# First modulation sums moved to TensorE, rotary tables moved to the start

## The chip, the core and the metric

The kernel runs on one core of a Trainium2 chip. A core has TensorE (matrix products, called PE in the profile, with its weight loads as PEld), VectorE (DVE), ScalarE (ACT), GpSimd (POOL) and SyncE (SP), which here only issues DMA transfers. Each engine takes its own instructions in the order in which they are written and waits where an operand is not ready. The metric is the device time of one execution in microseconds (us), and the kernel is compared by the median of its runs.

## The reference, cut to what matters

A two-layer encoder trunk, sequence 512, model width 1024, all in fp32. Each layer first makes six modulation vectors from the conditioning vector c, then normalises the input, and reads it with one input projection that feeds three mixers:

```
c_act = jax.nn.silu(c)
for l in range(DEPTH):
    mod = c_act @ w_mod[l] + b_mod[l]
    sh1, sc1, g1, sh2, sc2, g2 = (m[:, None, :] for m in jnp.split(mod, N_MOD, axis=-1))
    h = rmsnorm(x, norm1[l]) * (1.0 + sc1) + sh1
    u = h @ w_in[l]
    ...
    x = x + g1 * (mixed @ w_out[l])
    h2 = rmsnorm(x, norm2[l]) * (1.0 + sc2) + sh2
    x = x + g2 * conv_ffn(h2, ffn_w_up[l], ffn_conv_w[l], ffn_conv_b[l], ffn_w_down[l])
```

`mod` has 6144 values per layer, 48 chunks of 128. Chunks 0 to 7 are the shift `sh1` and chunks 8 to 15 the scale `sc1`: no column of `h` can be made before its shift and its scale are there. Two of the mixers also need rotary tables, the cosines and sines of `positions` times fixed frequencies.

## The kernel before, in words

The activations lie transposed: the model dimension on 128 partitions in 8 rows of blocks (k = 0 to 7, `KD`), the 512 tokens along the columns. A product in full precision is made of three products of fp32r parts (`mm3`, lines 348 to 350): each weight tile is split into a high part `wh` (a cast on ScalarE, line 342) and a low part `wl` (a subtraction, line 343, on VectorE or GpSimd), and `h` likewise into two tiles named `t`.

The program is written as one text; a scheduler lays down the order of each engine from priorities (`PRI`, `low`, `after`) and its own costs. That order is fixed when the kernel is built.

What runs at the start of layer 0:

- `x` (tile `xs`), the columns of small parameters (`cols`), the constants (`cst`, in two parts, the first 265 KB on ScalarE's queue) and c (`crow`, on one partition) are loaded. c is activated on one partition and copied to all 128 by two products with ones (`spread`, tile `cb`, line 296) into `cact`.
- `x_norm` squares the 8 rows of `xs` on ScalarE (`nsq`, line 412), adds them on VectorE (`nacc`, line 421), sums over partitions on TensorE (`ssq`, line 391), takes the root on VectorE (`rs_y`, lines 356 to 365) and spreads it over the partitions by four transposes (`bc`, line 372).
- The first projection (`proj(0)`, six column blocks) goes over k. For each k, `make_h` makes two modulation sums by `mod_chunk`: a tile `rawm` of 512 KB (the weights of one chunk, transposed in memory) is multiplied by `cact` and summed along its columns in one VectorE instruction (line 327), which gives one column of `modv`. Three buffers serve `rawm`. Then the gain `g_n` (line 771), `ht` (line 440, VectorE), the high part of `t` (line 442, ScalarE) and its low part (line 443, VectorE). 18 products `u` per k follow.
- When the last k is done, six blocks of `u` are read out, four of them squared and summed (`dsq`, line 843). Beside the second projection (`proj(1)`, five blocks) run the preparation of the state-space mixer (lines 497 to 637) and the rotary tables: `rope_tables` (lines 466 to 488) loads the positions and makes `tabA`, `tabS` and `tabC` on VectorE, with four sines on ScalarE.

The weights of the projections are loaded to `raw` (three buffers), and SP issues the transfers of `rawm`, `raw` and the others in one fixed order: a transfer that waits for a buffer holds up all behind it. The PSUM tiles `ssq`, `bc` and others share two banks; `bc` keeps one of them until the last `ht` of layer 0's first projection.

The other 80 modulation sums are made later by the same VectorE instruction.

Of the kernel before, what the change touches and what calls it, by code (L numbers as in the profile page):

```python
# [20 lines left out]
D = 1024  # L21
# [3 lines left out]
PRI = {"xs": -400, "U1": 300, "ws": -200, "rs": -300, "cu": 10, "fin": 20, "glu": -30, "par": -30,  # L25
       "prep1": -20, "qk": 20, "rope": -20}
MK = 2
OWN = 6
TOGETHER = 300
DQ = (0, 3, 0, 0)  # L30
BLOCKS = ((0, 8), (8, 15), (15, 22))
EPS = 1e-6
# [23 lines left out]
for _name, _w in (  # L56
    ("ident", 128), ("ss", 12), ("fr", 6), ("nidx", 256), ("mf", 128), ("mb", 128),
    ("rz", 256), ("sel", 128), ("bias", 896),
):
    CONST[_name] = (_n, _w)  # L60
    _n += _w
# [9 lines left out]
def _constants():  # L71
    out = np.zeros((128, NCONST), np.float32)

    def put(name, a):
        o, w = CONST[name]
        out[:, o:o + w] = a

    p = np.arange(128)
    put("ident", np.eye(128))
    sel = np.zeros((128, 128))  # L80
    for j in range(32):
# [50 lines left out]
def _layout(inp):  # L132
    a = {k: np.asarray(v) for k, v in inp.items()}
    f = np.float32
    o = {}
    o["xT"] = a["x"][0].T.reshape(8, 128, N).transpose(1, 0, 2)
    o["c"] = a["c"].reshape(1, D)
    o["pos"] = a["positions"].reshape(1, N)
    o["const"] = _constants()
    o["wmod"] = a["w_mod"].transpose(0, 2, 1).reshape(L, 48, 128, D)  # L140
    cols = np.zeros((128, L, NCOL), f)
    rope = lambda g: np.concatenate([g[:16], g[16:], g[16:], g[:16]])
# [74 lines left out]
def program(ctx, tc, a, out):  # L217
# [41 lines left out]
    xs = keep.tile([128, KD, N], F32, name="xs")  # L259
    crow = strm.tile([128, 1024], F32, tag="raw", name="crow", bufs=3)  # L260
    S.dma_start(crow[:1], a["c"])
    nc.sync.dma_start(cols, a["cols"])
    for k in range(0, KD, 2):
        nc.sync.dma_start(xs[:, k:k + 2], a["xT"][:, k:k + 2])
    S.dma_start(cst[:, :NEARLY], a["const"][:, :NEARLY])

# [19 lines left out]


    cact = keep.tile([128, D], F32, name="cact")
    S.activation(cact[:1], crow[:1], AF.Tanh, scale=0.5)
    V.scalar_tensor_tensor(cact[:1], cact[:1], 1.0, crow[:1], add, mul)  # L290

    def spread():
        for i in range(2):
            o = ps("cb", "big")
            c = slice(i * 512, i * 512 + 512)
            T.matmul(o, K("mf")[:1], cact[:1, c], start=True, stop=True)
            S.copy(cact[:, c], o)

# [10 lines left out]

    def mod_chunk(l, j, pooled=False):  # L310
        with low("mod" if l or j >= 16 else "mod0"):
            mod_chunk_(l, j, pooled)

    def mod_chunk_(l, j, pooled=False):
        if cur["modraw"]:
            p_, nb = cur["modraw"]
            r = p_.tile([128, 1024], F32, tag="rawm", name="rawm", bufs=nb)
            nc.sync.dma_start(r, a["wmod"][l, j])
        else:
            r = raw_tile(a["wmod"][l, j], 1024)  # L320
        if pooled:
            G.tensor_tensor(r, r, cact, mul)
            acc = tiny("modacc", 1, bufs=4)
            S.activation(r, r, AF.Copy, scale=0.5, accum_out=acc)
            G.tensor_tensor(modv[l][:, j:j + 1], acc, col(l, "bmod", j), add)
        else:
            V.tensor_tensor_reduce(out=r, in0=r, in1=cact, scale=0.5, scalar=col(l, "bmod", j),  # L327
                                   op0=mul, op1=add, accum_out=modv[l][:, j:j + 1])

# [418 lines left out]
    def mixing(l, background):  # L748
# [7 lines left out]
        if l == 0:  # L756
            g1 = keep.tile([128, 8], F32, name="g_n10")
            start = startup(pst)
            with low("par"):
                next(start, None)  # L760
            *_, R = x_norm(slice(0, N), True)
            ready = cur["rs"]
            cur["H"] = [(ht(2 * k), ht(2 * k + 1)) for k in range(KD)]
        H = cur["H"]

        def make_h(k):
            with after(*[cur["ht"]] if k else ()):
                mod_chunk(0, 8 + k)
            with after(cur["ht"] if k else ready):
                mod_chunk(0, k)  # L770
            V.tensor_scalar(g1[:, k:k + 1], modv[0][:, 8 + k:9 + k], 1.0, col(0, "n1", k), op0=add, op1=mul)
            normed(R, g1, modv[0][:, 0:8], k, slice(0, N))
# [7 lines left out]
        def proj(gi, o):  # L780
# [3 lines left out]
            for k in range(KD):  # L784
# [3 lines left out]
                for i0 in range(0, nt, 3):  # L788
                    i1 = min(nt, i0 + 3)
                    wh, wl = split(r[:, i0 * 128:i1 * 128], (i1 - i0) * 128,  # L790
                                   G if (i0 == 0 or l + gi == 0) else V)
                    for i in range(i0, i1):
                        c = slice((i - i0) * 128, (i - i0) * 128 + 128)
                        mm3(o[i], (wh[:, c], wl[:, c]), H[k], k == 0, k == KD - 1)
# [86 lines left out]
        with ExitStack() as st:  # L881
            if l == 0:
                cur["modraw"] = (pool("early", "right", st), 3)
            if l:
# [16 lines left out]
        if l == 0:  # L901
# [11 lines left out]
            pst.close()  # L913
            with low("rope"):
                rope_tables()
        dil_roots(0, 32)
# [557 lines left out]
    banks("pa", cur["pst"], big=6, ps=2)  # L1474
    spread()
    open_norm()
# [33 lines left out]
```

## Time and profile before

| | |
|---|---|
| median of 3 runs | 1508.67 us (1507.85 to 1509.09) |
| the profiled execution | 1506.77 us, span 1505.0 us |
| TensorE busy | 1385.0 us, 92% of the span |
| VectorE busy | 1070.4 us, 71% |
| ScalarE busy | 693.3 us, 46% |
| GpSimd busy | 373.0 us, 25% |
| mean granted TensorE clock | 0.959 of full |

The span is that of one execution. The shares are averages over all stages; the change touches the first 140 us or so, in which the engines stand differently. The chain of waits follows the work that ended last back through whatever released it, so a piece of it is time in which nothing else could have finished the kernel sooner.

### The profile page before, as it was taken

What the parts mean: (1) busy time and instruction counts of PE and PEld (TensorE: products, weight loads), DVE (VectorE), ACT (ScalarE), POOL (GpSimd) and SP (SyncE); (2) the same over time, 40 slices, a digit from 0 to 9 for tenths busy, and PEclk for the clock granted to TensorE, in tenths of its full rate; (3) what the DMA queues carried; (4) which work ended last, traced back from release to release, by engine and by line L of the source; (5) the groups of instructions that cost most, each with busy time, mean ns of one, the idle gap of its engine ahead of it and who ended that gap; (6) DMA issues with size and microseconds to landing.
All of it is one profiled execution on the core that took longest, in us unless ns stands there. A gap on an engine that the chain in (4) does not pass through costs nothing.

```text
span 1505.0 us, 20265 instructions
## 1 busy us (share of the span) xinstructions
PE 1385.0 (92%) x7160; PEld 1116.8 (74%) x7160; DVE 1070.4 (71%) x2117; ACT 693.3 (46%) x1347; POOL 373.0 (25%) x322
## 2 busy tenths in 40 slices
PE   5879689888899999999998889898899999999998
PEld 3657556657878878887888777566698888888887
DVE  8996977865798789788656588767558663663663
ACT  4464255653454433544456334666445442442441
POOL 2566541220212152243234433323101000000000
PEclk9999888989999999999999989999899999999999
DMA  7665313203647377477336342000032333323322
GB/s 257 193 198 176 120 33 107 99 1 104 214 154 241 110 243 248 138 226 238 111 95 200 103 132 72 26 18 10 2 116 65 98 98 98 98 89 107 97 90 93
DMA packets 79111, 185.09 MB, mean 123 GB/s; under 512 B 12705, under 2 KB 37793, under 8 KB 79010
## 3 DMA queue, kind: packets, MB, share of 16 engines
q1 hardware_dynamic: 77712, 181.43, 38.2%
q10 hardware_dynamic: 1298, 2.37, 0.4%
q8 instruction: 56, 0.92, 0.3%
q14 instruction: 45, 0.37, 0.1%
HBM read 165.95 MB, written 15.73 MB: 121 GB/s over the span
## 4 chain that ended last, share of the span: by engine, by line
PE 65%; DVE 19%; DMA 4%; issue 4%; POOL 3%; ACT 3%; SPq 1%; DVEq 0%; ACTq 0%; POOLq 0%
PE up L349 9%; PE up L350 9%; PE up L348 9%; PE dn L350 5%; PE dn L349 5%; PE dn L348 5%; DVE rawm L327 3%; PE pv L1078 3%; PE pt L1060 2%; DMA rawm<-in_wmod 2%; PE wo L348 2%; PE wo L349 1%; PE wo L350 1%; PE u L349 1%; DVE wl L343 1%
## 5 line engine op out<-in xcount | busy, mean ns | idle before, releaser
L342 ACT CAST wh<-raw 128x512 fp32r<-128x512 f32 (+3 forms) x400 | 223.5, 567 | 305.8 <-PE dn L350 120.6
L348 PE MATMUL up<-t,wh 128*128 128x512 f32 (+1 forms) x736 | 279.4, 381 | 2.5 <-ACT t L442 2.2
L349 PE MATMUL up<-t,wl 128*128 128x512 f32 (+1 forms) x736 | 279.4, 381 | 2.0 <-DVE wl L343 1.9
L350 PE MATMUL up<-t,wh 128*128 128x512 f32 (+1 forms) x736 | 278.2, 381 | 1.2 <-DVE t L443 1.2
L343 DVE TENSOR_TENSOR wl<-raw,wh 128x512 fp32r<-128x512 f32 (+3 forms) x296 | 202.0, 686 | 105.7 <-ACT wh L342 105.3
L343 POOL TENSOR_TENSOR wl<-raw,wh 128x384 fp32r<-128x384 f32 (+1 forms) x104 | 135.9, 1308 | 276.5 <-ACT wh L342 268.9
L349 PEld LDWEIGHTS up<-t,wl 128*128 128x128 f32 x736 | 138.1, 188 | 31.1 <-DVE wl L343 3.7
L348 PEld LDWEIGHTS up<-t,wh 128*128 128x128 f32 x736 | 138.3, 188 | 30.0 <-ACT t L442 3.7
L350 PEld LDWEIGHTS up<-t,wh 128*128 128x128 f32 x736 | 137.3, 188 | 28.7 <-DVE t L443 2.4
L349 PE MATMUL dn<-gh,wl 128*128 128x512 f32 (+1 forms) x366 | 140.7, 386 | 2.0 <-DVE wl L343 2.0
L348 PE MATMUL dn<-gh,wh 128*128 128x512 f32 (+1 forms) x366 | 141.2, 387 | 0.0
L350 PE MATMUL dn<-gl,wh 128*128 128x512 f32 (+1 forms) x366 | 140.8, 386 | 0.0
L327 DVE CUSTOM_DVE_ANT_0 rawm<-rawm,cact,cols 128x1024 f32<-128x1024 f32 x84 | 115.4, 1376 | 15.1 <-DMA rawm<-in_wmod 15.1
L349 PE MATMUL u<-t,wl 128*128 128x512 f32 (+1 forms) x248 | 98.0, 396 | 8.3 <-POOL wl L343 4.4
L348 PE MATMUL u<-t,wh 128*128 128x512 f32 (+1 forms) x248 | 97.8, 399 | 4.8 <-ACT t L442 2.6
L350 PE MATMUL u<-t,wh 128*128 128x512 f32 (+1 forms) x248 | 95.6, 393 | 4.2 <-DVE t L443 4.0
L1056 ACT ACTIVATE P<-P,nb 128x512 f32<-128x512 f32 x96 | 69.1, 721 | 34.3 <-DVE nb L1054 29.1
L349 PEld LDWEIGHTS dn<-gh,wl 128*128 128x128 f32 x366 | 68.8, 188 | 15.9 <-DVE wl L343 2.8
L348 PEld LDWEIGHTS dn<-gh,wh 128*128 128x128 f32 x366 | 68.8, 188 | 14.4 <-ACT gh L1399 1.1
L350 PEld LDWEIGHTS dn<-gl,wh 128*128 128x128 f32 x366 | 68.5, 188 | 13.9 <-DVE gl L1400 1.3
L1060 PE MATMUL pt<-cst,P 128*128 128x128 f32 x384 | 63.4, 293 | 4.1 <-ACT P L1056 3.4
L1419 DVE SCALAR_TENSOR_TENSOR xs<-dn,modv,xs 128x512 f32<-128x512 f32 (+1 forms) x50 | 36.2, 727 | 41.3 <-PE dn L350 41.3
(441 smaller groups left out, 2784.2 us busy)
## 6 DMA issues: line engine op xcount, KB each, us to landing
raw<-in_w_up SPq DMA_DIRECT2D x88, 512.0 KB, 3.7
rawm<-in_wmod SPq DMA_DIRECT2D x84, 512.0 KB, 4.4
raw<-in_w_dn SPq DMA_DIRECT2D x32, 448.0 KB, 3.3
raw<-in_w_dn SPq DMA_DIRECT2D x16, 512.0 KB, 3.6
raw<-in_w_in SPq DMA_DIRECT2D x40, 192.0 KB, 2.6
raw<-in_wmod SPq DMA_DIRECT2D x12, 512.0 KB, 3.6
raw<-in_w_in SPq DMA_DIRECT2D x16, 320.0 KB, 3.7
s5wcp<-s5d SPq DMA_DIRECT2D x8, 640.0 KB, 5.7
```

The lines of the kernel that those rows point to most:

```text
L327: V.tensor_tensor_reduce(out=r, in0=r, in1=cact, scale=0.5, scalar=col(l, "bmod", j), op0=mul, op1=add, accum_out=modv[l][:, j:j + 1])
L342: S.copy(hi[:, :n], src)
L343: (eng or V).tensor_tensor(lo[:, :n], src, as32(hi[:, :n]), sub)
L348: T.matmul(o, wh, xh, start=first, stop=False)
L349: T.matmul(o, wl, xh, start=False, stop=False)
L350: return T.matmul(o, wh, xl, start=False, stop=last).ins
L1056: S.activation(P, P, AF.Exp, scale=-1.0, bias=nb, accum_out=sums)
L1060: T.transpose(t_ps[:, c], P[:, c], ident)
L1078: T.matmul(o[hh * 64:hh * 64 + 64], v[:, k, c0:c0 + 64], PT[hh][:, k], start=(first and k == 0), stop=(last and k == 3))
L1419: return V.scalar_tensor_tensor(xs[:, m, c], o, modv[l][:, 40 + m:41 + m], xs[:, m, c], mul, add).ins
```

## The change

Five edits, all at the start of layer 0.

1. The first 16 modulation sums (chunks 0 to 15) are made by TensorE, four at a time (`mod_quad`). The weights lie in memory untransposed, 1024 by 512 for four chunks (the pairs of `QUADS`: 8, 9, 0, 1, then 10, 11, 2, 3, and so on), in four loads of 512 KB to the same three `rawm` buffers. c, activated and repeated 32 times (`cw`), is the stationary operand: eight fp32 products of 32 columns by 512, the product for block k in the column tile of partitions 32(k mod 4). The sums of the four column tiles are copied to `mrow` (ScalarE) and added and turned to columns by four products with the column `pick`; two VectorE instructions add the bias.
2. `make_h` calls it for every second k, so that two rows of `ht` follow one group of sums.
3. c is loaded as a 128 by 8 tile (`ccol`) and activated there. `cact`, which the later sums still need, is made by eight transposes behind the second projection.
4. `rope_tables` is called ahead of `x_norm`, with its load of the positions ahead of `xs`.
5. The low parts of the first projection's weights are made by VectorE instead of GpSimd.

The core of the diff:

```
-    crow = strm.tile([128, 1024], F32, tag="raw", name="crow", bufs=3)
-    S.dma_start(crow[:1], a["c"])
-    nc.sync.dma_start(cols, a["cols"])
+    ccol = keep.tile([128, KD], F32, name="ccol")
+    S.dma_start(ccol, a["c"])
     for k in range(0, KD, 2):
         nc.sync.dma_start(xs[:, k:k + 2], a["xT"][:, k:k + 2])
+    nc.sync.dma_start(cols, a["cols"])
...
+    cth = keep.tile([128, KD], F32, name="cth")
+    S.activation(cth, ccol, AF.Tanh, scale=0.5)
...
     def spread():
         for i in range(2):
-            o = ps("cb", "big")
-            c = slice(i * 512, i * 512 + 512)
-            T.matmul(o, K("mf")[:1], cact[:1, c], start=True, stop=True)
-            S.copy(cact[:, c], o)
+            o = ps("cb")
+            for k in range(4):
+                T.transpose(o[:, k * 128:k * 128 + 128], cth[:, 4 * i + k:4 * i + k + 1].to_broadcast([128, 128]), ident)
+            S.copy(cact[:, i * 512:i * 512 + 512], o)
...
+    def mod_quad(q):
+        o = ps("mq")
+        p_, nb = cur["modraw"]
+        for t in range(4):
+            r = p_.tile([128, 1024], F32, tag="rawm", name="rawm", bufs=nb)
+            nc.sync.dma_start(r, a["wquad"][q, t])
+            for k in (2 * t, 2 * t + 1):
+                T.matmul(o[k % 4 * 32:k % 4 * 32 + 32], cur["cw"][:, k], r[:, k % 2 * 512:k % 2 * 512 + 512],
+                         start=k < 4, stop=k >= 4)
+        row = p_.tile([128, 512], F32, tag="mrow", name="mrow")
+        S.copy(row, o)
+        o = ps("mc")
+        for j in range(4):
+            T.matmul(o[:, j:j + 1], row[:, j * 128:j * 128 + 128], K("pick"), start=j == 0, stop=j == 3)
+        for j in (0, 2):
+            d = QUADS[q][j]
+            V.tensor_tensor(modv[0][:, d:d + 2], o[:, j:j + 2], col(0, "bmod", d, 2), add)
...
             with low("par"):
                 next(start, None)
+            with low("rope"):
+                rope_tables()
             *_, R = x_norm(slice(0, N), True)
...
         def make_h(k):
-            with after(*[cur["ht"]] if k else ()):
-                mod_chunk(0, 8 + k)
-            with after(cur["ht"] if k else ready):
-                mod_chunk(0, k)
-            V.tensor_scalar(g1[:, k:k + 1], modv[0][:, 8 + k:9 + k], 1.0, col(0, "n1", k), op0=add, op1=mul)
+            if k % 2 == 0:
+                mod_quad(k // 2)
+                V.scalar_tensor_tensor(g1[:, k:k + 2], modv[0][:, 8 + k:10 + k], 1.0, col(0, "n1", k, 2), add, mul)
             normed(R, g1, modv[0][:, 0:8], k, slice(0, N))
...
-                                   G if (i0 == 0 or l + gi == 0) else V)
+                                   G if i0 == 0 and l + gi else V)
...
             pst.close()
-            with low("rope"):
-                rope_tables()
+            with low("spread"):
+                spread()
```

The order that the scheduler lays down changes at three places that matter here. (The new program is 24 lines longer, so its line numbers are higher: the squares are line 433 instead of 412, `ssq` 412 instead of 391, `bc` 393 instead of 372, `u` 369 to 371 instead of 348 to 350.)

ScalarE at the start, before, from the first square on (`sn` and `cs` belong to the state-space mixer, L297 is the spread of c):

```order
L412 ACTIVATE nacc<-xs 128x512
L412 ACTIVATE nsq<-xs 128x512 x2
L514 ACT_TABLE_LOAD
L514 ACTIVATE sn<-th 128x16
L515 ACTIVATE cs<-n,halfpi 128x16
L412 ACTIVATE nsq<-xs 128x512
L297 COPY cact<-cb 128x512
L412 ACTIVATE nsq<-xs 128x512 x2
L297 COPY cact<-cb 128x512
L412 ACTIVATE nsq<-xs 128x512 x2
```

ScalarE at the start, now; ahead of these rows stand the same first three squares, a table load and the first sine of `tabA`, and a table load and `dt`:

```order
L506 ACT_TABLE_LOAD
L506 ACTIVATE tabA<-tabA,halfpi 32x512
L523 ACT_TABLE_LOAD
L523 ACTIVATE mg<-m 128x16
L524 ACTIVATE im<-m 128x16
L525 ACTIVATE rho_75<-m 128x16
L535 ACT_TABLE_LOAD
L535 ACTIVATE sn<-th 128x16
L536 ACTIVATE cs<-n,halfpi 128x16
L506 ACTIVATE tabC<-tabC,halfpi 128x512
L508 ACTIVATE tabS<-tabS,cst 128x512
L433 ACTIVATE nsq<-xs 128x512 x2
```

All sines of the tables, and the small functions of the state-space preparation, now stand between the third and the fourth square.

TensorE from the root on, before (`ssq` sums the squares, `bc` spreads the root, `u` are projection products):

```order
L391 MATMUL ssq<-cst,nacc 128x1 x4
L372 MATMUL bc<-cst,rs_yr 128x128 x4
L348 MATMUL u_258<-t_237,wh 128x512
L349 MATMUL u_258<-t_237,wl 128x512
L348 MATMUL u_259<-t_237,wh 128x512
```

TensorE from the root on, now (`mq` are the products of the sums, `mc` those that turn them to columns):

```order
L412 MATMUL ssq<-cst,nacc 128x1 x4
L393 MATMUL bc<-cst,rs_yr 128x128 x4
L340 MATMUL mq<-rawm,cw 32x512 x8
L346 MATMUL mc<-cst,mrow 128x1 x4
L340 MATMUL mq<-rawm,cw 32x512 x2
L369 MATMUL u_283<-t_260,wh 128x512
L370 MATMUL u_283<-t_260,wl 128x512
```

The sums' products stand behind `bc` and ahead of the projection. After each 36 products `u` (two rows) the next six or seven `mq` and four `mc` follow in the same way.

SP's queue of transfers, before, from the load of `xs` on:

```order
L264 DMA xs<-in_xT 128x1024 x4
L318 DMA rawm<-in_wmod 128x1024 x2
L303 DMA raw<-in_w_in 128x768
L318 DMA rawm<-in_wmod 128x1024 x2
L303 DMA raw<-in_w_in 128x768 x3
L318 DMA rawm<-in_wmod 128x1024
```

SP's queue of transfers, now, from the same place:

```order
L268 DMA xs<-in_xT 128x1024 x4
L269 DMA cols<-in_cols 128x632
L338 DMA rawm<-in_wquad 128x1024 x3
L310 DMA raw<-in_w_in 128x768 x3
L927 DMA cst<-in_const 128x1408
L310 DMA raw<-in_w_in 128x768 x2
L338 DMA rawm<-in_wquad 128x1024 x5
L310 DMA raw<-in_w_in 128x768
L338 DMA rawm<-in_wquad 128x1024 x3
```

The first three weight tiles of the sums are loaded at once; the fourth, first of the five, waits for one of the three buffers, and the sixth projection weight stands behind those five.

## Rows read from the trace of the kernel before

**Rows 1.** Chain of waits, 25 to 120 us: start, duration in us, engine, tile, line.
```profile
33.88 1.20 DVE rawm L327
...
38.64 0.75 DVE ht L440
39.39 1.20 DVE rawm L327
...
75.22 0.60 DVE tabA L480
...
119.54 0.23 PE u L350
```

**Rows 2.** Timeline of TensorE: start us, us, engine, line, output and inputs, count.
```profile
6.44 3.77 PE L296 MATMUL cb<-cact,cst 1*128 1x512 f32 x4 [6.44 <-DVE cact L290]
...
68.37 0.95 PE L843 MATMUL dsq<-cst,sqd 128*128 128x2 f32 x8
...
80.93 1.83 PE L617 MATMUL tps<-cp,bp 128*128 128x128 f32 x14
...
231.77 1.95 PE L1078 MATMUL pv<-pt,vb 128*64 128x256 f32 x16
```

**Rows 3.** Busy time: stretch, length, PE, PEld, DVE, ACT, POOL, granted clock, DMA, GB/s.
```profile
25.45:68.37 42.92, 38.70 (x145) 28.77 (x145) 41.74 (x60) 15.08 (x27) 24.00 (x20) 0.96 0.74 236
60.00:63.00 3.00, 1.61 (x6) 0.67 (x4) 3.00 (x4) 1.02 (x2) 3.00 (x5) 1.00 0.41 83
63.00:67.00 4.00, 3.45 (x9) 2.73 (x10) 4.00 (x5) 1.99 (x4) 2.81 (x2) 0.57 0.02 4
68.40:134.00 65.60, 54.40 (x288) 43.13 (x287) 49.98 (x93) 41.10 (x88) 39.16 (x36) 0.95 0.57 176
```

**Rows 4.** VectorE by line, 69 to 106 us: count, busy us, mean ns, idle before.
```profile
L480 DVE SCALAR_TENSOR_TENSOR tabA<-ht,tabA 128x512 f32<-128x512 f32 x3 | 2.5, 832 | 0.0
...
L481 DVE TENSOR_SCALAR tabA<-tabA 128x512 f32<-128x512 f32 x1 | 0.4, 416 | 0.0
```

**Rows 5.** Timeline of all engines, 0 to 26 us.
```profile
1.29 0.36 ACTq L265 DMA_DIRECT2D cst<-in_const  x1
...
6.97 0.63 ACT L412 ACTIVATE nsq<-xs 128x512 f32<-128x512 f32 x1 [0.18 <-DMA xs<-in_xT]
...
7.62 1.28 ACT L514 ACT_TABLE_LOAD   x1
...
8.91 0.22 ACT L514 ACTIVATE sn<-th 128x16 f32<-128x16 f32 x1
...
16.96 1.87 PE L391 MATMUL ssq<-cst,nacc 128*128 128x1 f32 x8 [6.74 <-DVE nacc L421]
...
18.86 0.16 DVE L394 TENSOR_SCALAR rv<-ssq 128x4 f32<-128x4 f32 x1 [1.54 <-PE ssq L391]
...
19.30 0.93 DVE L357 TENSOR_SCALAR rs_yr<-rs_yr 128x4 int32<-128x4 int32 x1
...
22.67 1.12 PE L372 MATMUL bc<-cst,rs_yr 128*128 128x128 f32 x4 [3.85 <-DVE rs_yr L365]
...
25.45 0.79 PE L348 MATMUL u<-t,wh 128*128 128x512 f32 x1 [1.66 <-ACT t L442]
```

**Rows 6.** Tile tabS, 60 to 130 us: count, minimum, median, maximum in ns, when.
```profile
L480 DVE SCALAR_TENSOR_TENSOR tabS<-ht,tabS x3: 682/685/1129, 76.7 to 98.0; 128x512 f32<-128x512 f32 x3
...
L487 ACT ACTIVATE tabS<-tabS,cst x1: 725/725/725, 106.2 to 106.2; 128x512 f32<-128x512 f32 x1
```

**Rows 7.** DMA issues: count, KB each, median us from issue to landing.
```profile
cst<-in_const ACTq DMA_DIRECT2D x1, 265.0 KB, 4.5
...
raw<-in_wmod SPq DMA_DIRECT2D x12, 512.0 KB, 3.6
```

**Rows 8.** Groups by line and shape, 0 to 69 us.
```profile
L343 POOL TENSOR_TENSOR wl<-raw,wh 128x384 fp32r<-128x384 f32 x17 | 21.7, 1282 | 36.4 <-ACT wh L342 36.3
...
L342 ACT CAST wh<-raw 128x384 fp32r<-128x384 f32 x17 | 8.5, 512 | 24.8 <-PE u L350 15.2 <-DMA raw<-in_w_in 7.3 <-POOL wl L343 2.3
L440 DVE SCALAR_TENSOR_TENSOR ht<-xs,g_n,bc 128x512 f32<-128x512 f32 x8 | 6.0, 745 | 0.2
```

More of the change, by code (lines that the diff above doesn't have):

```diff
@@ L25 @@
 PRI = {"xs": -400, "U1": 300, "ws": -200, "rs": -300, "cu": 10, "fin": 20, "glu": -30, "par": -30,
-       "prep1": -20, "qk": 20, "rope": -20}
+       "prep1": -20, "qk": 20, "rope": -20, "spread": -30}
 MK = 2
@@ L30 @@
 DQ = (0, 3, 0, 0)
+QUADS = tuple((8 + 2 * q, 9 + 2 * q, 2 * q, 2 * q + 1) for q in range(4))
 BLOCKS = ((0, 8), (8, 15), (15, 22))
@@ L56 @@
 for _name, _w in (
-    ("ident", 128), ("ss", 12), ("fr", 6), ("nidx", 256), ("mf", 128), ("mb", 128),
+    ("ident", 128), ("ss", 12), ("pick", 1), ("fr", 6), ("nidx", 256), ("mf", 128), ("mb", 128),
     ("rz", 256), ("sel", 128), ("bias", 896),
@@ L79, in _constants @@
     put("ident", np.eye(128))
+    put("pick", (p % 32 == 0).astype(np.float32)[:, None])
     sel = np.zeros((128, 128))
@@ L136, in _layout @@
     o["xT"] = a["x"][0].T.reshape(8, 128, N).transpose(1, 0, 2)
-    o["c"] = a["c"].reshape(1, D)
+    o["c"] = a["c"].reshape(8, 128).T
     o["pos"] = a["positions"].reshape(1, N)
@@ L140, in _layout @@
     o["wmod"] = a["w_mod"].transpose(0, 2, 1).reshape(L, 48, 128, D)
+    w = a["w_mod"][0].reshape(D, 48, 128)
+    o["wquad"] = np.stack([w[:, list(q)].reshape(4, 2, 128, 512).transpose(0, 2, 1, 3).reshape(4, 128, 1024)
+                           for q in QUADS])
     cols = np.zeros((128, L, NCOL), f)
@@ L285, in program @@
     G.memset(epsc, EPS)
+    cth = keep.tile([128, KD], F32, name="cth")
+    S.activation(cth, ccol, AF.Tanh, scale=0.5)
+    V.scalar_tensor_tensor(cth, cth, 1.0, ccol, add, mul)
+    V.tensor_scalar(cth, cth, 0.5, None, op0=mul)
     cact = keep.tile([128, D], F32, name="cact")
-    S.activation(cact[:1], crow[:1], AF.Tanh, scale=0.5)
-    V.scalar_tensor_tensor(cact[:1], cact[:1], 1.0, crow[:1], add, mul)
     def spread():
         for i in range(2):
-            o = ps("cb", "big")
-            c = slice(i * 512, i * 512 + 512)
-            T.matmul(o, K("mf")[:1], cact[:1, c], start=True, stop=True)
-            S.copy(cact[:, c], o)
+            o = ps("cb")
+            for k in range(4):
+                T.transpose(o[:, k * 128:k * 128 + 128], cth[:, 4 * i + k:4 * i + k + 1].to_broadcast([128, 128]), ident)
+            S.copy(cact[:, i * 512:i * 512 + 512], o)
     modv = [keep.tile([128, 48], F32, name=f"modv{l}") for l in range(L)]
@@ L308, in low, with mod_chunk, mod_chunk_ @@
         return tc.high_priority(-n) if n else ExitStack()
-    def mod_chunk(l, j, pooled=False):
+    def mod_chunk(l, j):
         with low("mod" if l or j >= 16 else "mod0"):
-            mod_chunk_(l, j, pooled)
-    def mod_chunk_(l, j, pooled=False):
+            mod_chunk_(l, j)
+    def mod_chunk_(l, j):
         if cur["modraw"]:
@@ L320, in mod_chunk_ @@
             r = raw_tile(a["wmod"][l, j], 1024)
[L321 to L328, printed above, removed]
+        V.tensor_tensor_reduce(out=r, in0=r, in1=cact, scale=1.0, scalar=col(l, "bmod", j),
+                               op0=mul, op1=add, accum_out=modv[l][:, j:j + 1])
+    def mod_quad(q):
[15 more added lines that the diff above has]
+            V.tensor_tensor(modv[0][:, d:d + 2], o[:, j:j + 2], col(0, "bmod", d, 2), add)
     def after(*ins):
@@ L882, in mixing @@
             if l == 0:
-                cur["modraw"] = (pool("early", "right", st), 3)
+                early = pool("early", "right", st)
+                cur["modraw"] = early, 3
+                cur["cw"] = early.tile([128, KD, 32], F32, name="cw")
+                V.tensor_copy(cur["cw"], cth.unsqueeze(2).to_broadcast([128, KD, 32]))
             if l:
@@ L1474, in program @@
     banks("pa", cur["pst"], big=6, ps=2)
-    spread()
     open_norm()
```

## The prediction

> **What bounds the kernel now.** I read the chain of waits first. Between the first projection product at 25.45 us [rows 5] and the squares' sums that follow the first projection (the first dsq, 68.37 us [rows 2]), it runs from one VectorE reduction of a modulation chunk to the next: rawm, ht, rawm [rows 1]. In those 42.92 us VectorE is busy 41.74 and TensorE 38.70 [rows 3]. So VectorE sets the pace, by a little. Its reductions of about 1.2 us [rows 1], two per row of weights, are the largest item, but the 144 products of 0.23 us [rows 1] are 33.4 us and stay. At most 9.5 us can be won here, even if VectorE cost nothing. From 68.4 to 134 us VectorE is busy 49.98 of 65.60 us [rows 3], and part of that is the rotary tables: twelve groups, 11.9 us together, of which the first and the last are shown [rows 4]. Ahead of 25.45 us stands one chain: ScalarE's squares, VectorE's adds, ssq (16.96), the root, bc (22.67) [rows 5]. What delays this chain delays everything behind it.
>
> **The change, part by part.** I carry one marker, the first dsq, and then the stretch behind it.
>
> *A. The squares, +10.0 us.* The tables' VectorE work now stands ahead of the adds, and ScalarE's sines ahead of the fourth square. The tables need the early constants: issued at 1.29 us [rows 5], 4.5 us to land [rows 7], so 5.8. Up to the clamp of the first table stand seven steps with a scalar, like that clamp 0.42, and six of 0.685 [rows 4, 6]: 7.05 us; starts overlap a little, so I take 12.7. ScalarE then works through: sine 0.72, four table loads of 1.28, dt 0.22, cosine 0.72, three small exponentials 0.41, two small sines 0.40, tabC and tabS 0.73 each; the durations are those of the load, the small sine and tabS [rows 5, 6]. That is 9.1 us: 21.8. (Before, one load stood among the squares.) Five squares 0.6 apart [rows 5] and three weight casts of 0.5 [rows 8] are left, then the last add of 0.69: ssq starts at 27.0 instead of 16.96.
>
> A load here costs what its row says: the square before it ends at 7.60, the load starts at 7.62 and takes 1.28, the sine starts at 8.91 [rows 5]. The Trainium skill (ScalarE: Activation LUTs, What ACT_TABLE_LOAD costs) counts a drain of about 1.38 us on top; by that, four loads would add some 5.5 us. The trace shows no such gap, so the sum goes without it.
>
> *B. The root, -1.0 us.* From ssq to bc it is 5.71 us now. One of its steps on 4 columns takes 0.93 us (and a second one nearly as much) while GpSimd works on low parts; its first step takes 0.16 [rows 5]. GpSimd no longer has these low parts: 1.5 us less. One low part (0.5) now stands in the chain on VectorE. bc starts at 27.0 + 4.7 = 31.7.
>
> *C. From bc to the first projection product, +10.0 us.* This is 2.78 us now. The first four sums are a new chain. Their eight products stand behind bc on TensorE, and only three of the four weight tiles have a buffer. The fourth load waits on SP until the first tile's products are done; queued behind it are the loads of the next four sums and of the sixth projection weight. bc takes 1.12 [rows 5]: 32.8. First products, cold, two passes of 0.85 (the old spread, four passes in 3.77 us) [rows 2]: 34.5. A load of 512 KB takes 3.6 us [rows 7]: 38.1. Last products 1.7 and a tail of 0.2: 40.0. Copy 0.6. The column products are eight passes like ssq, 1.87 cold [rows 5]. Two adds and a gain 0.5, ht 0.74 [rows 8], t like a sine of its shape 0.72 [rows 6]. The first projection product starts at 44.5 instead of 25.45.
>
> *D. The projection, +15.6 us.* The sums' products stand between the bursts of the projection, not beside them: after each 36 projection products TensorE does the next sums, then waits for copy, column products, adds, ht and t. How much four column tiles overlap, no row shows. The nearest is pv, two 64-wide tiles: 16 passes of 256 columns in 1.95 us, 0.122 each, where full-width passes of 128 columns take 0.131 (14 in 1.83) [rows 2]. Two tiles go at the price of one. So a 512-column product costs 0.49 instead of some 0.85, and six cost 2.9. A gap is 2.9 + 0.2 + 0.57 + 0.9 (column products, warm) + 0.45 + 0.74 + 0.72 = 6.5 us. In the third group the fourth tile again waits for a buffer that comes free only behind the projection: 0.5 + 3.6 + 1.0 + 3.6 for the rest of the gap = 8.7. Three gaps: 21.7.
>
> After a stretch in which TensorE worked 1.61 of 3 us, its clock fell: granted 0.57 in the next 4 us, so mostly 1.2 instead of 2.4 GHz [rows 3], and nine products ran there that take 0.23 us each at full clock. That is some 1.7 us; I give each of the four bursts half of it, 3.4. Sum 33.4 + 21.7 + 3.4 = 58.5 us against 42.92: first dsq at 103.0.
>
> The Trainium skill (TensorEngine Tiling (Array Packing), Theoretical Speedup) allows four times for 32-wide tiles. By that a gap would be 1.4 us shorter and the sum about 3.4 us smaller. The pv row agrees with its twofold for 64-wide tiles and says nothing of 32.
>
> VectorE's 16 low parts I cost at nothing: in 14 to 15 us per two rows it has four of them, ht, t and the adds, some 7 us. A low part takes GpSimd 1.28 [rows 8]; VectorE's price for this shape has no row, and I bound it by zero and that 1.28. Without cover they would cost up to 1.28 x 16 = 20 us; I take none of it. The bytes of the sums are the same; the rest of the constants loads earlier, ahead of weights that are needed only after 50 us, and costs nothing while these wait.
>
> *E. Behind the first dsq, -11 us.* The tables are gone from VectorE: 11.9 us of work [rows 4]; nine of their pieces, 6.1 us, stand on the chain of waits, the first at 75.22 [rows 1]. GpSimd's memsets and the first rotary products move forward too. Ends: 0, and -14 (TensorE works 54.40 of 65.60 us, a few of them at half clock) [rows 3]. I take -11, near the work itself.
>
> *F. The spread of the activated c, +1 us.* Two products and two copies at the start had cover from the loads. Eight transposes (four take 1.12 us cold as bc [rows 5], so eight about that warm) and two copies now stand near the end of the second projection, where TensorE is nearly full. Ends: 0 and 2.2.
>
> Sum: +10.0 - 1.0 + 10.0 + 15.6 - 11 + 1 = +24.6 us. The profiled execution took 1506.77 us (span 1505.0); the median of the runs is 1508.67, and to that I add the difference: 1533. Behind the second projection each engine does the same work in nearly the same order, so the delay is carried to the end.
>
> **The rivals.**
> 1. *Column tiles do not overlap.* Products then cost 0.85 warm and 1.7 cold. The gaps grow by 2.2, 1.0 and 2.2, and in the first group six cold products outlast the load, about +8.5: 1547. Against it: the pairs in pv. Chance 0.13.
> 2. *The cheap ends together.* Full overlap of four tiles (-3.4), no half clock (-3.4), relief at its end of -14: 1523. For it: VectorE's nearly full rows behind 68 us. Chance 0.15.
> 3. *The relief decides, and it is faster.* If the sums' products ran under the loads, ahead of bc, and each gap were shorter than 2.5 us ((42.9 - 33.4 - 1.9) / 3, with one half-clock burst), TensorE alone would bound the projection: first product at 25.5, first dsq near 64, then -11: about -15, 1494. The point from which it decides is ssq: starting before about 17 us. Against it: the order puts bc ahead of all sums and ScalarE's sines ahead of the squares. Chance 0.06.
> 4. *Nothing measurable.* The delay ahead of the first dsq would have to be absorbed behind it, where only 14 us can be. Chance 0.03.
>
> **How the numbers follow.** My own case, 1523 to 1543, has 0.63. About 0.2%, 3 us, is what a measurement of this kernel can tell from no change. Faster than that has rival 3's 0.06, no change 0.03, slower the rest, 0.91. The range reaches past rival 2, for a start shorter than worked out, and past rival 1: 1514 to 1551.
>
> **What would show it.** In the new profile: ScalarE with six table loads ahead of the fourth square, ssq at about 27 (A); bc near 32 (B); the first projection product near 44 (C); between bursts of 36 products gaps of 6 to 9 us in which TensorE waits for a load, the copy, ht and t, the third the longest (D); first dsq near 103; from there to the end of the second projection some 55 us instead of 66 (E). I am wrong at the root if ssq starts before 20 us, or if projection products run while sums are still being computed.

## The result, and the profile after

The changed kernel takes 1542.51 us (median of 4 runs, 1540.84 to 1544.26), the kernel before, run beside it, 1508.26. The ratio is 1.023, 95% interval 1.0212 to 1.0248: slower, as forecast; the predicted time was 1533 us, in a range of 1514 to 1551. The profiled execution took 1544.26 us, span 1542.4.

First TensorE in the timeline of the changed kernel, 26 to 110 us, cut at the dots: of the projection products only the first of each burst of 36 is shown (start us, us, engine, line, tile, count, in brackets the wait and its end; the count of `mq` is in passes, two to a product):

```profile
28.59 1.87 PE L412 MATMUL ssq<-cst,nacc 128*128 128x1 f32 x8 [28.59 <-DVE nacc L442]
33.22 1.11 PE L393 MATMUL bc<-cst,rs_yr 128*128 128x128 f32 x4 [2.77 <-DVE rs_yr L386]
34.27 3.05 PE L340 MATMUL mq<-rawm,cw 128*32 128x512 f32 x12
40.02 1.92 PE L340 MATMUL mq<-rawm,cw 128*32 128x512 f32 x4 [2.71 <-DMA rawm<-in_wquad]
42.63 1.86 PE L346 MATMUL mc<-cst,mrow 128*128 128x1 f32 x8 [0.69 <-ACT mrow L343]
...
46.71 0.80 PE L369 MATMUL u<-t,wh 128*128 128x512 f32 x1
...
56.74 1.91 PE L340 MATMUL mq<-rawm,cw 128*32 128x512 f32 x12
...
61.56 1.02 PE L340 MATMUL mq<-rawm,cw 128*32 128x512 f32 x2 [1.11 <-DMA rawm<-in_wquad]
62.51 0.50 PE L369 MATMUL u<-t,wh 128*128 128x512 f32 x1
...
71.16 1.90 PE L340 MATMUL mq<-rawm,cw 128*32 128x512 f32 x10
76.03 1.05 PE L340 MATMUL mq<-rawm,cw 128*32 128x512 f32 x4 [2.97 <-DMA rawm<-in_wquad]
...
81.91 0.80 PE L369 MATMUL u<-t,wh 128*128 128x512 f32 x1
...
91.46 1.91 PE L340 MATMUL mq<-rawm,cw 128*32 128x512 f32 x12
...
97.63 0.50 PE L369 MATMUL u<-t,wh 128*128 128x512 f32 x1 [2.46 <-ACT t L463]
...
107.55 0.95 PE L864 MATMUL dsq<-cst,sqd 128*128 128x2 f32 x8
```

Against [rows 1, 2, 5]: the squares' sums start 11.6 us later, `bc` 10.6, the first projection product 21.3, the first `dsq` 39.2. Between the bursts lie gaps of 5.8, 10.7 and 6.2 us. TensorE's own work for a group of sums is small; what stands around it is not. Now these stretches as busy time (columns as in [rows 3]): from the place of the first product before to its place now, the projection, in it the second gap with the first products behind it, and what lies behind the projection up to the first `ssa`, the squares' sums behind the second projection:

```profile
25.45:46.71 21.26, 11.60 (x41) 5.26 (x41) 8.25 (x35) 3.79 (x8) 0.00 (x0) 0.84 0.43 136
46.71:107.55 60.84, 51.71 (x214) 35.41 (x213) 24.01 (x49) 17.66 (x32) 5.03 (x5) 0.89 0.40 127
71.16:82.70 11.54, 7.47 (x29) 3.22 (x29) 3.37 (x8) 2.48 (x4) 0.00 (x0) 0.78 0.56 183
107.55:168.52 60.97, 53.60 (x293) 43.48 (x292) 35.73 (x71) 37.77 (x84) 33.69 (x35) 0.94 0.60 192
```

The projection takes 60.84 us instead of 42.92, at a granted clock of 0.89 instead of 0.96 [rows 3], and VectorE is busy for only 24.01 of them: no engine sets the pace, a chain does. The last row has its counterpart in the kernel before from the first `dsq` to the first `ssa`:

```profile
68.37:133.40 65.03, 53.83 (x284) 42.60 (x283) 49.41 (x93) 40.67 (x88) 38.56 (x36) 0.95 0.56 175
```

VectorE has lost 13.7 us of work there, the stretch only 4.1. The first `ssa` is 35.1 us late, and the end of the span 37.4.

### The profile page after: what moved, and what is told of

Its sections match the earlier page's. It is cut to its first block, busy times and chain, and to the rows that moved or that the text cites. A ratio compares the mean times of both kernels' runs of the same rounds, so it can differ in the third digit from the quotient of the medians.

```text
span 1542.4 us, 20445 instructions
## 1 busy us (share of the span) xinstructions
PE 1402.1 (91%) x7260; PEld 1120.8 (73%) x7260; DVE 1042.3 (68%) x2107; ACT 700.6 (45%) x1355; POOL 349.4 (23%) x306
## 4 chain that ended last, share of the span: by engine, by line
PE 68%; DVE 16%; DMA 5%; ACT 4%; issue 3%; POOL 3%; SPq 1%; DVEq 0%; ACTq 0%; POOLq 0%
PE up L370 9%; PE up L371 9%; PE up L369 9%; PE dn L371 5%; PE dn L370 5%; PE dn L369 5%; PE pv L1103 3%; PE u L370 2%; PE u L371 2%; PE pt L1085 2%; PE u L369 2%; DMA rawm<-in_wmod 1%; PE wo L369 1%; DVE rawm L328 1%; PE wo L370 1%
## 5 line engine op out<-in xcount | busy, mean ns | idle before, releaser
L364 DVE TENSOR_TENSOR wl<-raw,wh 128x512 fp32r<-128x512 f32 (+3 forms) x312 | 207.7, 669 | 132.3 <-ACT wh L363 131.9
L364 POOL TENSOR_TENSOR wl<-raw,wh 128x384 fp32r<-128x384 f32 (+1 forms) x88 | 114.0, 1298 | 244.5 <-ACT wh L363 240.7
L328 DVE CUSTOM_DVE_ANT_0 rawm<-rawm,cact,cols 128x1024 f32<-128x1024 f32 x68 | 92.7, 1366 | 13.8 <-DMA rawm<-in_wmod 13.5
L1081 ACT ACTIVATE P<-P,nb 128x512 f32<-128x512 f32 x96 | 69.3, 722 | 34.0 <-DVE nb L1079 29.4
L371 PEld LDWEIGHTS dn<-gl,wh 128*128 128x128 f32 x366 | 68.4, 188 | 15.6 <-DVE gl L1425 0.8
L1444 DVE SCALAR_TENSOR_TENSOR xs<-dn,modv,xs 128x512 f32<-128x512 f32 (+1 forms) x50 | 36.2, 727 | 43.9 <-PE dn L371 43.9
```

Of the source, the lines that this page charges most:

```text
L328: V.tensor_tensor_reduce(out=r, in0=r, in1=cact, scale=1.0, scalar=col(l, "bmod", j), op0=mul, op1=add, accum_out=modv[l][:, j:j + 1])
L364: (eng or V).tensor_tensor(lo[:, :n], src, as32(hi[:, :n]), sub)
L371: return T.matmul(o, wh, xl, start=False, stop=last).ins
L1081: S.activation(P, P, AF.Exp, scale=-1.0, bias=nb, accum_out=sums)
L1444: return V.scalar_tensor_tensor(xs[:, m, c], o, modv[l][:, 40 + m:41 + m], xs[:, m, c], mul, add).ins
```

## The experiments

The kernel before, run beside them, took 1501 to 1503 us, some 0.4% less than beside the changed kernel; so they are compared by ratio to it. Times inside a run come from its trace.

**e1, the tables back at their old place** (`rope_tables()` in front of `spread()` behind the second projection). 

> The changed kernel with the rotary tables called at their old place (and the positions loaded there); the sums stay on TensorE, the low parts on VectorE. Theory (A, C and D add up; the tables cost the start, the sums the projection): ssq starts near 17 us instead of 28.6; from bc to the first projection product it is still about 13.5 us and from there to the first dsq about 60 us, so first dsq near 96 us; the tables' VectorE work falls into the gaps of the projection, where VectorE has room, so most of the relief behind it stays: 1542.5 - 11.6 = about 1531 us, 1527 to 1536. Rival (the tables at the start are what costs, the sums on TensorE are nearly free): first dsq near 80 us or earlier, 1508 to 1518 us.

Measured: 1522.67 us, ratio 1.013 (1.0109 to 1.0152), 1.0 percentage point (15 us) below the changed kernel's.

```profile
11.85 1.87 PE L412 MATMUL ssq<-cst,nacc 128*128 128x1 f32 x8 [11.85 <-DVE nacc L442]
```

```profile
28.95:93.56 64.61, 55.74 (x215) 37.50 (x214) 32.24 (x66) 20.40 (x36) 9.19 (x10) 0.81 0.45 147
```

`ssq` starts 16.7 us earlier, 5 earlier even than in the kernel before: the other edits had made the start shorter (e5 has 1.1 us for the low parts, e9 another 2.2 for c as a 128 by 8 tile), and the tables took more than that away. First `dsq` 93.56 is near the theory's 96, but by two differences that partly cancel: `ssq` 5 us earlier than expected, and a projection of 64.6 us instead of some 60. It is 3.8 us longer than in the changed kernel, with 4.0 us more of TensorE's busy time at a granted clock of 0.81 against 0.89; why the clock is lower here, no run shows. Without the tables the sums, with the edits that come with them, still cost 25 us of the first `dsq`: both edits cost. The stretch behind the projection takes 61.1 us as in the changed kernel, with VectorE busy 35.8 us: the tables' work on VectorE now falls into the projection, as expected.

**e2, the kernel before with the tables alone moved.** 

> The kernel before with only the rotary tables called ahead of the squares. Theory (A, C and D add up): with two table loads among the squares instead of six, ssq starts 7 to 10 us later than 16.96, the projection keeps its 43 us and first dsq is 7 to 10 us later; 5 to 11 us come back behind it since VectorE is relieved there: 1508.3 + 9 - 8 = about 1509 us, 1504 to 1515. Rival (the tables at the start are what costs): over 1530 us.

Measured: 1507.89 us, ratio 1.0031 (1.0016 to 1.0045). `ssq` is at 28.13, 11.2 us later and more than expected, but the first product `u` at 35.05 and the first `dsq` at 75.8, 7.4 later. Of the difference 1.5 us come back in the root, which takes 4.21 us instead of 5.71 since no low part of GpSimd falls into it, and 2.2 in the projection, which takes 40.75 us: VectorE does not have its sums done earlier (three of the 16 start ahead of the first `u`, as before), but it has 2 us less of other work there, and the granted clock is 1.00 instead of 0.96; no run separates the two. So the tables at the start cost this kernel 5 us and the changed one 15. The changed kernel had more to lose: the tables delay its `ssq` by 16.7 us, from 11.85 (e1). Behind the projection (75.8 to the first `ssa` at 140.2):

```profile
75.80:140.20 64.40, 53.12 (x285) 43.40 (x284) 42.53 (x79) 38.10 (x84) 35.26 (x35) 0.95 0.57 179
```

6.9 us less on VectorE than before, and 0.6 us gained. That is the first sign against step E. (The traced execution, 1512.37 us, was the slowest of this run's ten.)

**e3, low parts on GpSimd again** (`G if (i0 == 0 or l + gi == 0) else V`). 

> The changed kernel with the low parts of the first projection's weights on GpSimd again. Theory (VectorE's low parts are hidden in the projection and worth 1.1 us in the root): ssq at 28.6 as it is, bc about 1 us later, gaps between bursts unchanged within 1 us each: 1541 to 1546 us. Rival (the 16 low parts on VectorE stand in the gaps of the projection, up to 1.28 us each): the projection gets 8 to 20 us shorter, 1523 to 1535 us.

Measured: 1553.51 us, ratio 1.0347 (1.0327 to 1.0367). A miss for both: slower still. In the trace the projection takes 59.9 us (60.84), so VectorE's low parts, at 557 ns each, cost at most 0.9 us there. `ssq` comes 1.0 us later and `bc` 0.55. The stretch behind takes 66.8 us instead of 60.97. The traced execution took 1544.9 us, the other four 1549.7 to 1555.2; what these lost besides no trace shows.

**e4, eight buffers for the weights of the sums** (`cur["modraw"] = early, 8`). 

> The changed kernel with eight buffers for the weights of the sums instead of three. Theory (the waits for a buffer are a term of their own in C and D): the waits of TensorE on a load of 2.71 us ahead of the first product, 1.11 and 2.97 us in the second and third gap vanish, nothing else does, gaps of 5 to 6 us stay: first dsq near 101 us, about 1536 us, 1533 to 1539. Rival (the clock decides the gaps: with shorter waits TensorE is also granted more): first dsq near 94 us, 1529 us. Third possibility (the loads only take their turn elsewhere, so the waits move to the projection's weights): within 2 us of 1542.5.

Measured: 1527.99 us, ratio 1.0172 (1.0146 to 1.0197). The waits for loads are gone, 4.1 us of them in the projection, and first `dsq` is at 96.17, 11.4 us earlier:

```profile
44.42:96.17 51.75, 46.28 (x207) 33.23 (x207) 22.49 (x47) 17.24 (x31) 11.30 (x8) 0.93 0.31 98
```

The projection is 9.1 us shorter; more than half of that, 5.4, is TensorE's busy time, and the granted clock rose from 0.89 to 0.93. About 1.0 of those 5.4 us are six passes of the second group that now stand ahead of the first `u`. The rival was nearer than the theory: where 4.1 us of waits went, 4.4 us of busy time went with them, at the higher clock.

**e6, the sums issued a pair of rows ahead**, eight buffers, tables late (`e` is the last product of row k; the sums may stand behind it at once, and their instructions have a higher priority):

```
+                        if l + gi == 0 and k % 2 == 0 and k < 6 and i == 5:
+                            mod_quad(k // 2 + 1, e)
```

> The sums on TensorE, but the products of the next four sums issued behind the first 18 projection products of the present pair of rows and not behind all 36; eight buffers for their weights; rotary tables called at their old place. Theory (the loss of the projection is the chain of sums, copy, ht and t between the bursts, and the cold clock behind it, not TensorE's work for the sums): no gaps, first projection product at 23 to 26 us, first dsq at 66 to 71 us as in the kernel before (33.4 of products, four times 2.5 + 1.1 for the sums), 61 us behind it instead of 65: 0 to 8 us faster than the kernel before, ratio 0.995 to 1.000. Rival (the loads decide: 2 MB of x, 8 MB for the sums and 3.1 MB of weights, at the 236 GB/s of the window of before some 56 us): TensorE waits for rawm in every quad, first dsq 75 to 82 us, ratio 1.003 to 1.007. Rival (the sums' work on TensorE is the loss): first dsq over 85 us.

Measured: 1507.22 us, ratio 1.0035 (1.0013 to 1.0056).

```profile
32.33 1.92 PE L339 MATMUL mq<-rawm,cw 128*32 128x512 f32 x16
35.22 0.95 PE L345 MATMUL mc<-cst,mrow 128*128 128x1 f32 x8
25.76:69.82 44.06, 44.06 (x217) 32.48 (x218) 25.91 (x52) 17.75 (x33) 9.28 (x7) 0.95 0.53 171
69.82:134.90 65.08, 57.52 (x296) 48.10 (x294) 49.04 (x89) 40.86 (x89) 37.98 (x37) 0.87 0.58 182
```

TensorE does not idle once in the projection. A group of sums costs it 1.92 + 0.95 = 2.9 us, and first `dsq` is at 69.82 against 68.37 before. So TensorE's work for the sums was not the loss; the place in its order and the loads were. This run changes both at once: against e1 its first `dsq` is 23.7 us earlier, and in e4 the eight buffers alone gave 11.4 to the changed kernel. The 4 us expected behind it did not come: VectorE has the tables there again and the clock is 0.87.

**e7, all eight products in one column tile** (`o[:32]` for `o[k % 4 * 32:k % 4 * 32 + 32]`). 

> The changed kernel with all eight products of a group of sums in one column tile of 32 instead of four. Theory (four column tiles overlap fully, as 12 passes in 1.91 us against 0.131 for a full-width pass of a quarter of the columns say): 16 passes then cost 0.5 us each warm and 0.9 cold, about 8 us a group instead of 2.5, partly under the waits for loads: first dsq 12 to 22 us later, 1555 to 1565 us where the changed kernel has 1542.5, ratio 1.030 to 1.038. Rival (a small stationary operand alone makes the product cheap, the tiles do not matter): within 2 us of the changed kernel, ratio 1.022 to 1.025.

Measured: 1544.89 us, ratio 1.0281 (1.0256 to 1.0306). Twelve passes, warm:

```profile
57.84 5.34 PE L340 MATMUL mq<-rawm,cw 128*32 128x512 f32 x12
```

5.34 us instead of 1.91: four tiles run 2.8 times as fast as one. First `dsq` is only 6.7 us later, between the two expectations: TensorE no longer waits for the loads of the sums (6.8 us in the changed kernel), and the clock in the projection is 0.94 instead of 0.89.

**e8, four buffers for the state-space matrices** (`name="bc", bufs=4`). 

> The changed kernel with four buffers instead of two for the state-space matrices (bc from in_s5b), so that all four loads are issued ahead of the writes they stood behind. Theory (behind the first dsq a chain of these transfers took the place of VectorE): the waits on bc from in_s5b at 132.7 and 136.0 us vanish and the stretch from the first dsq to the first ssa falls from 60.9 to 55 to 58 us: 3 to 6 us faster than the changed kernel, ratio 1.019 to 1.021. Rival (TensorE, busy 53.5 of 60.9 us, and the low parts bound it): 60 to 61 us, ratio 1.022 to 1.024.

Measured: 1542.22 us, ratio 1.0265 (1.0231 to 1.0299). VectorE's one wait on that load (1.9 us) is gone, and the stretch takes 60.6 us. The rival holds: these loads, though the chain of waits ran through them, did not set the end.

**e11, the second projection's low parts on VectorE too** (`G if i0 == 0 and l + gi > 1 else V`). 

> The changed kernel with the low parts of the second projection's weights on VectorE too. Theory (behind the first dsq GpSimd holds up the chain u, bp, bt of the state-space preparation and the low parts; VectorE, busy 35.7 of 60.9 us, has room): GpSimd loses some eight low parts of 1.28 us, VectorE gets eight of 0.55; the stretch from the first dsq to the first ssa falls from 60.9 to 56 to 59 us, ratio 1.019 to 1.022. Rival (TensorE with its 53.5 us busy and ScalarE's copies bound it): 60 to 62 us, ratio 1.022 to 1.025. Third (VectorE is the bound behind the first dsq, as the prediction's step E had it): 63 us or more.

Measured: 1541.51 us, ratio 1.0261 (1.0237 to 1.0285). The stretch shrinks as the theory said:

```profile
106.94:163.69 56.75, 50.90 (x294) 41.50 (x293) 35.97 (x77) 37.54 (x84) 26.97 (x28) 1.00 0.66 205
```

4.2 us less than in the changed kernel: 1.5 of waits, and 2.7 of TensorE's busy time, at a granted clock of 1.00 instead of 0.94. TensorE's waits in the stretch in the two traces (line waited for, us in total, times, longest), the changed kernel first:

```profile
PE btp L633 <- ACT bp L626: 2.4, 1, 2.4
PE tps L638 <- ACT bt L634: 2.3, 1, 2.3
PE u L370 <- DVE wl L364: 1.4, 1, 1.4
PE u L370 <- POOL wl L364: 1.2, 2, 0.6
```

```profile
PE u L370 <- DVE wl L364: 3.4, 4, 1.3
PE tps L638 <- ACT bt L634: 1.2, 1, 1.2
PE u L369 <- ACT wh L363: 0.8, 1, 0.8
PE tps L638 <- POOL u L621: 0.3, 1, 0.3
```

The whole time did not follow; the ratio is no better than the changed kernel's 1.023: 4.8 us gained at the first `ssa` are 1.1 at the end of the span. In this trace three later stretches are longer (first `ssa` to `pv` 70.4 us against 69.3, `pv` to `wo` 144.4 against 141.5, `up` to `dn` 99.1 against 97.1) and one is shorter (`wo` to `up` 64.1 against 66.2); why, no run here separates. The same holds of e3, 4.5 us late at the first `ssa` and 0.7 at the end: a few us at this marker cannot be told in the whole time.

**e5, the kernel before with the low parts alone on VectorE.** 

> The kernel before with only the low parts of the first projection's weights on VectorE instead of GpSimd. Theory (formed after the first four runs: the relief behind the first dsq comes from the low parts that leave GpSimd, not from the tables that leave VectorE): from the first dsq to the first ssa 60 to 62 us instead of 65.0; in the projection VectorE, busy 41.74 of 42.92 us, gets 16 low parts of 0.56 us, so first dsq about 9 us later; together +5 us, ratio about 1.003. Rival (step E of the prediction: the relief is the tables'): still 65 us behind the first dsq, +9 us, ratio about 1.006.

Measured: 1501.49 us, ratio 0.9987 (0.9966 to 1.0009): no difference. Neither theory saw how. First `dsq` is 3.7 us earlier (64.66; 1.8 of it ahead of the first `u`), not 9 later, and the stretch behind takes 69.2 us at a clock of 0.85, so my second theory fell here: low parts on VectorE bring no relief behind the projection by themselves. VectorE's rows in the projection, before, then e5:

```profile
L327 DVE CUSTOM_DVE_ANT_0 rawm<-rawm,cact,cols 128x1024 f32<-128x1024 f32 x14 | 21.3, 1520 | 0.0
L443 DVE SCALAR_TENSOR_TENSOR t<-ht,modv,t 128x512 fp32r<-128x512 f32 x8 | 8.9, 1115 | 1.0 <-ACT t L442 1.0
```

```profile
L327 DVE CUSTOM_DVE_ANT_0 rawm<-rawm,cact,cols 128x1024 f32<-128x1024 f32 x14 | 17.9, 1280 | 2.3 <-DMA rawm<-in_wmod 2.3
L343 DVE TENSOR_TENSOR wl<-raw,wh 128x384 fp32r<-128x384 f32 x14 | 7.7, 550 | 0.0
L443 DVE SCALAR_TENSOR_TENSOR t<-ht,modv,t 128x512 fp32r<-128x512 f32 x8 | 6.7, 843 | 0.1
```

With no low parts on GpSimd the same VectorE instructions take less: 3.4 + 2.2 us back for these two groups, against 7.7 paid; another 3.2 are pieces of the state-space preparation (`er`, `ei`), shorter and two fewer in this stretch. The two levels return in e2 with GpSimd's low parts (1522 and 1116 ns) and in e9 without (1277 and 839).

**e9, e10, e12, towards a faster kernel.** e9 is e5 with c as a tile. 

> The kernel before with two of the five edits: the low parts on VectorE, and c loaded and activated as a 128 by 8 tile, spread by eight transposes at the start; the sums stay on VectorE, the tables behind the first projection. Theory (the start was held by the activation of c on one partition and its copies: with the sums on TensorE and late tables ssq started at 11.8 us): ssq at 12 to 14 us instead of 15.8 in the run with the low parts alone, first projection product 20 to 22 us, the projection 41 us as there, first dsq 61 to 63; ratio 0.995 to 0.998. Rival (the first loads hold the projection's start): first product at 23 us or later and ratio 0.998 to 1.000.

Measured: 1505.76 us, ratio 1.0026 (1.0008 to 1.0043); `ssq` 13.57, first `u` 22.41, first `dsq` 66.75, a miss for both: VectorE paces the projection (TensorE waits 8.7 us for `t`), and the earlier start is lost.

e10 puts one group of four sums on TensorE, ahead of the projection. 

> As the run named e9, but the first four sums of the projection (for two rows) on TensorE, with five buffers, and the other 12 on VectorE. Theory (the sums on TensorE cost only where they stand between bursts; ahead of the projection TensorE is idle): the first projection product at 24 to 26 us (the fourth load lands about 21), VectorE has about 5 us less in the projection, which lasts 37 to 39 us: first dsq 62 to 64, ratio 0.995 to 0.998. Rival (the chain from load to t costs more than it saves): first product after 27 us, first dsq 66 or later, ratio 1.000 or above.

Measured: 1504.1 us, ratio 1.0022 (1.0004 to 1.004). First `u` 26.46 and first `dsq` 64.1, at the edge of what the theory had; its ratio did not come, since the stretch behind takes 68.0 us at a clock of 0.87.

e12 adds e11's low parts and 64 unused bytes (`keep.tile([128, 16], F32, name="pad")`). 

> As the run named e10 (first four sums on TensorE, the other 12 on VectorE, tables late), with the low parts of the second projection's weights on VectorE too (as in the run named e11), and 64 unused bytes per partition ahead of the weight buffers. In every run that has the new small tiles of c, a product of the last down projection took 395 ns instead of 390 and the 528 of them 275.4 us instead of 272.3; these tiles move wh and wl by 64 bytes against gh and gl, so that they differ by 64 modulo 128 where they were equal. Theory (the place of the weights against the moving operand sets it): with the 64 bytes the last down projection takes 272.3 us again. Rival (it is something else in those kernels): 275.4. For the rest: first dsq 62 to 65 us; if GpSimd's chain bounds the stretch behind it here too, first ssa 60 to 64 us later instead of 68; ratio 0.994 to 0.998. If VectorE, which has the tables in that stretch, bounds it: 68 us or more, ratio 0.999 to 1.001.

Measured: 1502.91 us, ratio 1.0003 (0.9986 to 1.002). The stretch behind takes 64.9 us, 3.1 less than in e10 and between the two expectations. The last down projection: 275.1 us, so its theory fell. No version beats the kernel before by more than the measurement can tell.

## Why the prediction was right or wrong

The order of the stages and most sizes came out as worked out. The time lies near the upper end of my own case and nearer to rival 1's 1547, which is chance, since that rival's condition does not hold.

| step | forecast us | measured us | by |
|---|---|---|---|
| A, squares | +10.0 | +11.6 | `ssq` 28.59 |
| B, root | -1.0 | -1.1 | `ssq` to `bc` 4.63 |
| C, to the first `u` | +10.0 | +10.7 | 13.49 |
| D, projection | +15.6 | +17.9 | 60.84 |
| E and F, behind it | -10 | -4.1 | 60.97 against 65.05 |
| carried to the end | 0 | +2.3 | span +37.4 |

**A** was right in kind: six table loads stand ahead of the fourth square. One of them, with its neighbours:

```profile
16.11 0.22 ACT L521 ACTIVATE dt<-cols 128x16 f32<-128x16 f32 x1
16.34 1.28 ACT L506 ACT_TABLE_LOAD   x1
17.64 0.72 ACT L506 ACTIVATE tabA<-tabA,halfpi 32x512 f32<-32x512 f32 x1
```

And the load of the constants in the chain of waits:

```profile
1.17 6.44 DMA cst<-in_const
```

The missing 1.6 us are mainly the constants: I took the 4.5 us of [rows 7], and they took 6.44. The Trainium skill's drain (ScalarE: Activation LUTs, What ACT_TABLE_LOAD costs) does not show: `dt` ends at 16.33 and the load starts at 16.34; that ends at 17.62 and the sine starts at 17.64.

**B** was right: GpSimd's low parts had slowed the root. In the kernel before, two of its steps take 0.93 and 0.92 us beside two low parts of GpSimd; in the changed kernel the same steps take 0.16. In e3 GpSimd's two low parts end before the root begins: its steps take 0.16 us again, and two VectorE steps just ahead of it 0.97 and 0.99.

**C and D** were right in their form: `bc`, then the sums, then `u`, with gaps between the bursts. The three gaps take 22.7 us together (forecast 21.7), the four bursts 38.1 (36.8). The longest gap, 10.7 us, is the second between bursts, that of the third group of sums, as the working had it; the list of signs called it the third. Two sizes erred in opposite directions. Products: I took two column tiles at the price of one from `pv` [rows 2]; four run nearly at once (1.91 us for 12 passes, 5.34 in e7), so rival 1 is out, and the overlap is 2.8 times where I took 2. The Trainium skill (TensorEngine Tiling (Array Packing), Theoretical Speedup) allows up to four times; the 2.8 of this trace lies below that. (By its own prices rival 1 adds some 6.6 us in the first group and not 8.5: eight products of 1.7 against the 7.0 that C has for products and load.) Clock: I gave 3.4 us for half-clock bursts, and the bursts cost 4.7 more than 33.4; the second gap with the start of its burst shows 0.78, and there the column products take 1.87 us against 1.05 in the other two. e4, without the waits for loads, gives back 4.4 us of busy time. e6 beside e1 shows that the gaps are what costs: the same sums and late tables, no gaps, first `dsq` 23.7 us earlier. How much of that is the order and how much the eight buffers, e6 does not show; by e4 the buffers would be about half.

VectorE's low parts cost next to nothing in the projection, as assumed (at most 0.9 us, e3).

**E** was the step that failed in size. I priced the relief by VectorE's work, 11.9 us, near its end of -14; it was -4.1 with F's eight transposes, some 1.4 us of TensorE. The work did go from VectorE, but TensorE waited for VectorE only in part. Its waits in the stretch, in the kernel before and then in e2, where 6.9 us of VectorE's work go and 0.6 are gained:

```profile
PE u L349 <- DVE wl L343: 3.8, 2, 2.9
PE u L349 <- POOL wl L343: 3.5, 3, 1.6
PE btp L612 <- ACT bp L605: 1.9, 3, 0.9
PE u L348 <- ACT wh L342: 1.6, 2, 0.9
```

```profile
PE u L349 <- POOL wl L343: 4.8, 3, 2.8
PE tps L617 <- ACT bt L613: 3.9, 2, 2.3
PE u L348 <- ACT wh L342: 1.6, 1, 1.6
PE btp L612 <- ACT bp L605: 1.0, 2, 0.8
```

The 3.8 us for VectorE's low parts are gone in e2, and the waits for GpSimd's low parts and for `bt` have grown by 4.9 together. In the changed kernel 7.3 us of waits are left (shown at e11) against 11.1 before, the larger part for `bp` and `bt`, which the state-space preparation makes through GpSimd, VectorE and ScalarE. e11 takes low parts off GpSimd and gains 4.2 us, 1.5 of them waits. That this chain holds the stretch is read from these waits; no run isolates it. e8 excludes the chain's loads from `in_s5b`; its writes and loads of `s5d` are moved in no run.

In these runs the relief of some 4 us comes only with two things together: the runs with 60 to 61 us there (the changed kernel, e1, e4, e7, e8) have VectorE down to 36 to 38 us in the stretch and the first projection's low parts off GpSimd. VectorE at 36.2 with these on GpSimd (e3) gives 66.8 us; low parts off GpSimd with VectorE at 49 to 53 (e5, e6, e9, e10) gives 65 to 69. The granted clock in these last four is 0.85 to 0.87, with 3 to 5 us more of TensorE's busy time than in the kernel before; in e12, which is e10 with the second projection's low parts off GpSimd as well, it is 0.95. What lowers it in some and not in the others is open.

**Carried to the end**: nearly, but not "the same work in the same time". The last down projection alone is 3.1 us longer, see the end; the other stages differ by up to 2.7 us either way.

Rival 2 (1523) was nearer on the overlap and wrong on clock and relief. Rival 3 would have needed sums ahead of `bc` and no gaps. e6 comes closest (`ssq` at 12.18, twelve of the first sixteen passes ahead of three of the four `bc`, no gaps): first `dsq` at 69.8, not 64, no relief behind it, and the time of the kernel before, not less.

## What to carry to other kernels

Work that moves from a busy engine to a fuller one is priced by where it stands in the new engine's order: here sums that take TensorE 2.9 us a group cost 25 us of the first `dsq` in a serial place with three buffers (e1), and 1.5 us issued one group ahead with eight (e6). Relief is priced by what the waiting engine waits for, not by the busy time that goes. And an instruction's duration is not its own: look at what runs on GpSimd beside VectorE, and at the clock behind each stall.

## What the runs showed of the hardware that was not expected

VectorE beside GpSimd: `rawm` 1520 ns against 1280, `t` 1115 against 843, with and without low parts on GpSimd (the kernel before and e5).

The last down projection takes 272.3 us in the kernel before, e2 and e5, and 275.1 to 275.4 in all others: every product of it takes a few ns longer, those of `up` do not. Before, the changed kernel, e12:

```profile
L350 PE MATMUL dn<-gl,wh x176: 387/389/472, 1228.8 to 1500.7; 128*128 128x512 f32 x176
```

```profile
L371 PE MATMUL dn<-gl,wh x176: 390/394/432, 1263.2 to 1538.1; 128*128 128x512 f32 x176
```

```profile
L372 PE MATMUL dn<-gl,wh x176: 390/393/425, 1222.1 to 1496.8; 128*128 128x512 f32 x176
```

The slower ones are all built from the changed kernel's text: they share the small tiles of c and a column more of constants (`pick`), which shift the buffers behind them, and the order of the first loads. 64 bytes more (e12) did not undo it. The cause is open.
